# A bidirectional mLSTM and Fourier encoder block on one core: longer scans in the gate chain, an earlier load of half of w_out, and the residual of the last layer written during its passes

## Chip, core and metric

One core of a Trainium2 chip runs the whole block. The metric is the device time of one execution in microseconds (us), as the median of several runs. All arithmetic is float32; the matmuls work on float32 values that were split into a rounded part and a remainder (below).

## What is computed

Sequence 1024, model width 1024, one layer. Of the reference, cut to what matters here:

```python
sh1, sc1, g1, sh2, sc2, g2 = split(silu(c) @ w_ada + b_ada, 6)
h = ln_plain(x) * (1 + sc1) + sh1
q, k, v, o, fz, gates = split(h @ w_in)
# mLSTM, 4 heads, forward and backward in time, chunks of 128 positions:
#   b = cumsum(log_f) in the chunk; running maximum of (log_i - b) in the chunk;
#   then a recurrence over the 8 chunks with state C, n, m
y = concat(mlstm(q, k, v, gates) * sigmoid(o), real(fft2(fz)))
x = ln_affine(ALPHA * x + (1 + g1) * (y @ w_out), ln1_g, ln1_b)
h2 = ln_plain(x) * (1 + sc2) + sh2
ff = square(relu(h2 @ w_ff1 + b_ff1)) @ w_ff2 + b_ff2      # width 4096 inside
return ln_affine(ALPHA * x + (1 + g2) * ff, ln2_g, ln2_b)
```

## The kernel before

**Matmuls.** Each product is three matmuls into one PSUM bank (`mm3`, lines L133, L134, L135): rounded times rounded, rounded times remainder, remainder times rounded. An operand is loaded raw, cast by ACT into its rounded part, and DVE (or POOL) subtracts to get the remainder. FF1 and FF2 multiply blocks by a scheme with fewer products: sums and differences of blocks are formed, and FF2 runs as seven passes, numbered 1, 2, 5, 6, 3, 7, 4, of 8 units each. A unit is a left and a right operand (`split_op`, L1204 cast, L1205 subtraction) and 24 matmuls. Left operands are read back from a DRAM buffer `hid_d` (`left`, L1221, on ACT's queue), right ones come from w_ff2 (`w2_raw`, L1212, on SP's queue).

**What sets the order.** The text is recorded first, and each engine's instructions are then put into an order by a scheduler; an engine and a queue work strictly in that order. `issue_after` ties an instruction to another. Tiles of one tag share a few places (`bufs`), so a load waits until the last reader of the tile that was there is done. The raw loads of all stages share the tag "raw" with three places in pool `xp`.

**The gate chain (L449 to L526).** Gates of 4 heads and 2 directions stand as rows of 64 x 1024 tiles: `I` (input gate), `Fz` (forget gate). DVE forms log-sigmoid, 16 scans for the cumulated sum in each chunk and direction (L468, L470), a subtraction (L472), 16 scans for the running maximum (L476, L478), small steps over the 8 chunk ends (L489 to L499), then L507 and L506. PE transposes the result of L506 (L522). Meanwhile PE multiplies V and other projections.

**The output projection (L864 to L895).** `wo_load` brings a 128 x 512 row block of w_out's second column half, one load, cast (L822) and subtraction (L823) each, eight in all. `acc_load` reads the residual x, `gate_rows(0, g1)` reads the row of the gate g1 (from `gr_d`) and the bias row b_ada and combines them (L680). `wo_pass` multiplies, then DVE scales the bank by g1 (L891) and adds it to `acc` (L892), which frees the bank. PE's order has the second column half of row blocks 1 and 3 (`woh`, `wol`) ahead of row block 4.

**The last layer.** After FF2's pass 1, `gate_rows(1, g2)` and `gb` (b_ff2 times g2, L1344) are formed, and eight instructions (L1347) set `acc[st] = ALPHA * x + gb`.

Of the kernel before, what the change touches and what calls it, by code (L numbers as in the profile page):

```python
# [22 lines left out]
NC = 8  # L23
# [9 lines left out]
ALPHA = 2.0 ** 0.25  # L33
# [57 lines left out]
def body(ctx, tc, x, c, w_ada, b_ada, w_in, b_gate, norm_w, w_out, ln1_g, ln1_b,  # L91
         w_ff1, b_ff1, w_ff2, b_ff2, ln2_g, ln2_b, cst, dft, out):
    nc = tc.nc
# [4 lines left out]
    wout = w_out.rearrange("o (kt p) n -> p (o kt) n", p=P)  # L98
# [18 lines left out]
    xes, xp = pool("xp", "left")  # L117
# [87 lines left out]
    pt = bank("c")  # L205
# [245 lines left out]
    for k_, dst in ((1, Fz), (0, I)):  # L451
        for hf in range(2):
            pt = bank("c")
            for i in range(4):
                nc.tensor.transpose(out=pt[0:64, i * P:(i + 1) * P], in_=zg[:, hf * 4 + i, k_, :], identity=ident)
            nc.vector.tensor_copy(out=dst[0:64, hf * 512:hf * 512 + 512], in_=pt[0:64, :])
    on = ones.broadcast_to([P, P])
    e_ = rowt("e_", 3)[0:64]
    Fr = Fz[0:64]
# [3 lines left out]
    nc.scalar.activation(out=e_, in_=e_, func=AF.Ln, bias=1.0)  # L463
    nc.vector.scalar_tensor_tensor(out=Fr, in0=Fr, scalar=0.0, in1=e_, op0=ALU.min, op1=ALU.subtract)
    br = e_
    for n in range(NC):
        f, r_ = slice(n * P, n * P + P), slice(n * P + P - 1, n * P - 1 if n else None, -1)
        nc.vector.tensor_tensor_scan(out=br[0:32, f], data0=on[0:32], data1=Fr[0:32, f], initial=0.0,  # L468
                                     op0=ALU.mult, op1=ALU.add)
        nc.vector.tensor_tensor_scan(out=br[32:64, r_], data0=on[32:64], data1=Fr[32:64, r_], initial=0.0,  # L470
                                     op0=ALU.mult, op1=ALU.add)
    nc.vector.tensor_sub(out=a_, in0=a_, in1=br)  # L472
    cm = Fr
    for n in range(NC):
        f, r_ = slice(n * P, n * P + P), slice(n * P + P - 1, n * P - 1 if n else None, -1)
        nc.vector.tensor_tensor_scan(out=cm[0:32, f], data0=a_[0:32, f], data1=a_[0:32, f], initial=-3e38,  # L476
                                     op0=ALU.max, op1=ALU.max)
        nc.vector.tensor_tensor_scan(out=cm[32:64, r_], data0=a_[32:64, r_], data1=a_[32:64, r_], initial=-3e38,  # L478
                                     op0=ALU.max, op1=ALU.max)
    G = a2.tile([64, NC], F32, name="G")  # L480
    bL = a2.tile([64, NC], F32, name="bL")
    ms = p0.tile([64, NC + 1], F32, name="ms")
# [19 lines left out]
    def bcn(t_):  # L502
        return t_.unsqueeze(2).broadcast_to([64, NC, P])

    a_v = a_.rearrange("p (n t) -> p n t", t=P)
    nc.vector.tensor_tensor(out=I[64:128].rearrange("p (n t) -> p n t", t=P), in0=a_v, in1=bcn(mx), op=ALU.subtract)  # L506
    nc.vector.tensor_tensor(out=cmv, in0=cmv, in1=bcn(m0), op=ALU.max)  # L507
    M = cm
    wi = rowt("wi", 0)[0:64]
    wiv = wi.rearrange("p (n t) -> p n t", t=P)  # L510
# [362 lines left out]
    def acc_load(st):  # L873
        nc.sync.dma_start(out=acc[st], in_=xv[:, st, :])

    for i in range(3):
        acc_load(i)
    gate_rows(0, g1)
    for kt in range(KT):
        wo_load(b1.tile([P, 512], F32R, name=f"woh{kt}"), b1.tile([P, 512], F32R, name=f"wol{kt}"), kt, 1, nc.vector)  # L880
    for i in range(3, NST):
        acc_load(i)

# [331 lines left out]
    nraw = [0]  # L1215

    def left(p, u):
        nraw[0] += 1
        pl, t_, n_ = ((r2, "hraw", 2), (opp, "op4", 2))[nraw[0] // 2 % 2] if nraw[0] > 2 else (xp, "raw", 3)
        raw = pl.tile([P, 2, 512], F32, name="hraw", tag=t_, bufs=n_)  # L1220
        nc.scalar.dma_start(out=raw, in_=hid_d[p - 1, 2 * u:2 * u + 2].rearrange("n p d -> p n d"))  # L1221
        return raw

    NU = NPR // 2
# [88 lines left out]
    for n_, p in enumerate((1, 2, 5, 6, 3, 7, 4)):  # L1313
        pbs = [bank(t_) for t_ in ("aabc", "abbc")[n_ % 2]]
        late = NLAST if p == 4 else 0
        for u in range(NU - late):
            ab = split_op(left(p, u), nc.vector), split_op(right(p, u), nc.vector)
            for i in range(4):
                mm_unit(pbs[i], i, u, ab)
            if p == 3:  # L1320
                raw = w2_raw(u, 1, 0)
                nc.vector.tensor_sub(out=tt[u], in0=raw, in1=tt[u])
            if p == 7 and u % 2:
                for ch in range(2):
# [12 lines left out]
        if n_ == 0:
            lg2, lb2 = [r2.tile([P, D], F32, name=n) for n in ("lg2", "lb2")]
            nc.sync.dma_start(out=lg2, in_=bc1(ln2_g))
            nc.sync.dma_start(out=lb2, in_=bc1(ln2_b))  # L1340
            gate_rows(1, g2)
            gb = xp.tile([P, D], F32, name="gb", tag="raw", bufs=3)
            nc.sync.dma_start(out=gb, in_=bc1(b_ff2))
            nc.vector.tensor_mul(out=gb, in0=gb, in1=g2)  # L1344
            for st in range(NST):
                nc.sync.dma_start(out=acc[st], in_=x2_d[st * P:st * P + P, :])
                nc.vector.scalar_tensor_tensor(out=acc[st], in0=acc[st], scalar=ALPHA, in1=gb, op0=ALU.mult,  # L1347
                                               op1=ALU.add)
# [25 lines left out]
```

## Time and profile before

| | |
|---|---|
| three runs | 1107.94, 1109.8, 1109.94 us; median 1109.8 |
| profiled execution | 1109.07 us, of it 1107.3 us from the first to the last instruction (the span), 1.8 us around it |
| PE (matmuls) | 1042.8 us busy, 94% |
| DVE / ACT / POOL | 775.9 (70%) / 469.4 (42%) / 319.6 us (29%) |
[...]

The engines: PE multiplies, DVE, ACT and POOL work elementwise, SP and ACT issue DMAs. A row of the timeline gives start, duration, engine, line, operation, output and inputs with shapes, a count, and in brackets the idle time before it and what ended it. [...] A busy PE at 0.50 does half the work.

### The profile page before, as it was taken

How to read it: one execution, taken by the hardware profiler on the slowest of the kernel's cores; microseconds unless marked ns; L12 is line 12 of the kernel's file. 1: busy time of each engine (PE TensorE's matmuls, PEld its weight loads, DVE VectorE, ACT ScalarE, POOL GpSimd, SP SyncE). 2: the span in 40 equal slices, each digit the busy share in tenths (PEclk: the TensorE clock that was granted, in tenths of full speed). 3: DMA queues.
4: the chain of work that ended last, by engine and by line, in shares of the span. 5: the costliest groups of instructions: out<-in, count | busy, mean ns of one | idle time of the engine just before them, and what ended most of it. 6: DMA issues, size and time to landing. Idle time of an engine off the chain costs nothing.

```text
span 1107.3 us, 14282 instructions
## 1 busy us (share of the span) xinstructions
PE 1042.8 (94%) x5033; PEld 857.1 (77%) x5033; DVE 775.9 (70%) x1431; ACT 469.4 (42%) x812; POOL 319.6 (29%) x247
## 2 busy tenths in 40 slices
PE   5899989999899898879999999999989999999995
PEld 3788978898677687668888888888868888888884
DVE  7943785967779488878565445445476896668997
ACT  3353125654355115676455445354344333333420
POOL 3554205532124011002777766752200000000000
PEclk7999989989899899989999999999999999999998
DMA  9926604432224802854566564546978885688402
GB/s 307 290 60 216 195 28 122 132 115 89 82 65 137 284 39 102 251 180 125 162 212 206 180 206 150 178 152 204 340 282 288 266 308 190 218 271 282 163 30 93
DMA packets 146887, 199.31 MB, mean 180 GB/s; under 512 B 9392, under 2 KB 74876, under 8 KB 146816
## 3 DMA queue, kind: packets, MB, share of 16 engines
q1 hardware_dynamic: 126688, 162.22, 44.7%
q10 hardware_dynamic: 20128, 36.18, 9.7%
q8 instruction: 39, 0.64, 0.2%
q14 instruction: 32, 0.26, 0.1%
HBM read 153.01 MB, written 45.36 MB: 179 GB/s over the span
## 4 chain that ended last, share of the span: by engine, by line
PE 57%; DVE 2%; ACT 1%; DMA 0%; issue 0%; DVEq 0%; ACTq 0%
PE psb L134 7%; PE psb L135 7%; PE psb L133 7%; PE psa L133 7%; PE psa L134 7%; PE psa L135 7%; PE psc L134 5%; PE psc L135 5%; PE psc L133 5%; DVE acc L1347 0%; PE psc L933 0%; DMA rw<-in_w_ff_dram 0%; DVE acc L1304 0%; ACT b L937 0%; ACT w L955 0%
## 5 line engine op out<-in xcount | busy, mean ns | idle before, releaser
L1204 ACT CAST o<-hraw 128x1024 fp32r<-128x1024 f32 x56 | 58.6, 1050 | 137.1 <-PE psc L135 107.5
L1205 DVE TENSOR_TENSOR o<-hraw,o 128x1024 fp32r<-128x1024 f32 x56 | 70.5, 1265 | 42.2 <-ACT o L1204 42.2
L133 PE MATMUL psa<-wh,hR 128*128 128x256 f32 (+2 forms) x268 | 81.0, 303 | 0.6 <-DVE acc L892 0.6
L135 PE MATMUL psa<-wh,hR 128*128 128x256 f32 (+2 forms) x268 | 79.9, 298 | 0.0
L134 PE MATMUL psa<-wl,hR 128*128 128x256 f32 (+2 forms) x268 | 79.4, 297 | 0.0
L134 PE MATMUL psa<-o,o 128*128 128x512 f32 x176 | 69.3, 394 | 5.9 <-DVE o L1205 5.9
L135 PE MATMUL psa<-o,o 128*128 128x512 f32 x176 | 69.4, 394 | 0.0
L133 PE MATMUL psa<-o,o 128*128 128x512 f32 x176 | 68.9, 393 | 0.0
L978 ACT ACTIVATE hq<-hq 128x512 f32<-128x512 f32 x59 | 37.1, 629 | 62.2 <-DVE hq L974 61.4
L134 PE MATMUL psb<-o,o 128*128 128x512 f32 x160 | 62.9, 393 | 0.0
L135 PE MATMUL psb<-o,o 128*128 128x512 f32 x160 | 62.8, 393 | 0.0
L133 PE MATMUL psb<-o,o 128*128 128x512 f32 x160 | 62.4, 392 | 0.0
L263 POOL TENSOR_TENSOR wl<-raw,wh 128x256 fp32r<-128x256 f32 (+2 forms) x27 | 38.0, 1430 | 73.8 <-ACT wh L262 73.8
L133 PEld LDWEIGHTS psa<-wh,hR 128*128 128x128 f32 x268 | 52.6, 196 | 2.7 <-DVE acc L892 1.3
L134 PEld LDWEIGHTS psa<-wl,hR 128*128 128x128 f32 x268 | 52.6, 196 | 2.0 <-issue 0.9
L135 PEld LDWEIGHTS psa<-wh,hR 128*128 128x128 f32 x268 | 52.4, 196 | 1.0
L1047 DVE TENSOR_TENSOR ws<-raw,ws 128x1024 fp32r<-128x1024 f32 x30 | 39.6, 1333 | 13.8 <-ACT ws L1046 13.8
L418 POOL TENSOR_TENSOR m<-m,mraw 128x512 f32<-128x512 f32 x28 | 39.5, 1412 | 29.6 <-ACT m L415 10.3
L1037 POOL TENSOR_TENSOR raw<-raw 128x512 f32<-128x512 f32 x15 | 21.3, 1418 | 90.4 <-DVE w L1112 86.2
L1204 ACT CAST o<-raw 128x1024 fp32r<-128x1024 f32 x32 | 33.3, 1048 | 31.4 <-DVE raw L1247 18.2
L1171 POOL TENSOR_TENSOR hq<-hq 128x512 f32<-128x512 f32 x16 | 22.7, 1418 | 78.1 <-ACT hq L979 62.1
L134 PEld LDWEIGHTS psa<-o,o 128*128 128x128 f32 x176 | 33.3, 189 | 13.7 <-DVE o L1205 6.3
(437 smaller groups left out, 3150.6 us busy)
## 6 DMA issues: line engine op xcount, KB each, us to landing
raw<-in_w_ff_dram SPq DMA_DIRECT2D x104, 512.0 KB, 4.8
hraw<-hid_d ACTq DMA_DIRECT2D x56, 512.0 KB, 4.8
hid_d<-hq SPq DMA_DIRECT2D x107, 256.0 KB, 3.2
mraw<-in_w_ada_dram SPq DMA_DIRECT2D x32, 512.0 KB, 4.2
raw<-in_w_in_dram SPq DMA_DIRECT2D x10, 512.0 KB, 3.9
xt<-in_x_dram SPq DMA_DIRECT2D x8, 512.0 KB, 5.3
wa<-in_w_ada_dram SPq DMA_DIRECT2D x16, 256.0 KB, 5.2
wa<-in_w_ada_dram SPq DMA_DIRECT2D x8, 512.0 KB, 8.1
```

Source lines behind the costliest of these rows:

```text
L133: nc.tensor.matmul(out=out_ap, lhsT=lh, rhs=rh, start=first, stop=False)
L134: nc.tensor.matmul(out=out_ap, lhsT=lh, rhs=rl, start=False, stop=False)
L135: return nc.tensor.matmul(out=out_ap, lhsT=ll, rhs=rh, start=False, stop=last)
L263: nc.gpsimd.tensor_sub(out=wl, in0=raw, in1=wh)
L418: nc.gpsimd.tensor_add(out=mc, in0=mc, in1=rv[:, i])
L978: nc.scalar.activation(out=h_, in_=h_, func=AF.Relu)
L1037: eng.tensor_add(out=r1[:, hi], in0=r1[:, lo], in1=r1[:, hi])
L1047: nc.vector.tensor_sub(out=w_[:, 1], in0=s_, in1=w_[:, 0])
L1171: nc.gpsimd.tensor_add(out=sa, in0=h12, in1=h22)
L1204: nc.scalar.copy(out=o_[:, 0], in_=raw)
L1205: eng.tensor_sub(out=o_[:, 1], in0=raw, in1=o_[:, 0])
```

## The change

Three places are edited. In the gate chain the 32 scans of 32 x 128 become 4 of 32 x 1024: a tile `keep` (two planes of 64 x 1024, set by POOL) holds, as the multiplier or addend of each position, 1 and 0 (sum) or 0 and -3e38 (maximum), so that the scan starts anew at each chunk. Two of the four copies at L456 go from DVE to ACT, and the maximum with m0 is tied behind the subtraction of mx. In the output projection four loads of two row blocks each replace eight of one; three of them stand ahead of the residual and the gate row. In FF2 the residual is written inside passes 2 and 5, `gb` has a tile of its own, `lb2` takes its place before pass 6, and `left` issues on SP's queue from its fourth call on, with other places.

```diff
@@ gate chain
-            nc.vector.tensor_copy(out=dst[0:64, ...], in_=pt[0:64, :])
+            (nc.vector.tensor_copy if k_ else nc.scalar.copy)(out=dst[0:64, ...], in_=pt[0:64, :])
...
-    for n in range(NC):
-        f, r_ = slice(n * P, n * P + P), slice(n * P + P - 1, n * P - 1 if n else None, -1)
-        nc.vector.tensor_tensor_scan(out=br[0:32, f], data0=on[0:32], data1=Fr[0:32, f], initial=0.0,
-                                     op0=ALU.mult, op1=ALU.add)
-        nc.vector.tensor_tensor_scan(out=br[32:64, r_], ...)
+    keep = md.tile([64, 2, S], F32, name="keep")
+    for w_, (rest, start) in enumerate(((1.0, 0.0), (0.0, -3e38))):
+        nc.gpsimd.memset(keep[:, w_], rest)
+        nc.gpsimd.memset(keep[:, w_].rearrange("p (n t) -> p n t", t=P)[:, :, 0:1], start)
+
+    def scans(out, src, which, initial, op0, op1):
+        for rs, r_ in ((slice(0, 32), slice(None)), (slice(32, 64), slice(None, None, -1))):
+            nc.vector.tensor_tensor_scan(out=out[rs, r_], data0=keep[rs, which], data1=src[rs, r_], initial=initial,
+                                         op0=op0, op1=op1)
+
+    scans(br, Fr, 0, 0.0, ALU.mult, ALU.add)
     nc.vector.tensor_sub(out=a_, in0=a_, in1=br)
     cm = Fr
-    for n in range(NC):
...
+    scans(cm, a_, 1, -3e38, ALU.add, ALU.max)
...
-    nc.vector.tensor_tensor(out=I[64:128]..., in0=a_v, in1=bcn(mx), op=ALU.subtract)
-    nc.vector.tensor_tensor(out=cmv, in0=cmv, in1=bcn(m0), op=ALU.max)
+    i_op = nc.vector.tensor_tensor(out=I[64:128]..., in0=a_v, in1=bcn(mx), op=ALU.subtract)
+    with tc.issue_after(i_op.ins):
+        nc.vector.tensor_tensor(out=cmv, in0=cmv, in1=bcn(m0), op=ALU.max)
@@ output projection
+    wor = {}
+    def wo_raw(j):
+        wor[j] = xp.tile([P, 2, 512], F32, name="wraw", tag="raw", bufs=3)
+        nc.sync.dma_start(out=wor[j], in_=wout[:, 2 * j:2 * j + 2, 512:1024])
+    for j in range(3):
+        wo_raw(j)
...
     for i in range(3):
         acc_load(i)
+    for kt in range(KT):
+        if kt == 6:
+            wo_raw(3)
+        a_, b_ = [b1.tile([P, 512], F32R, name=f"wo{n_}{kt}") for n_ in "hl"]
+        nc.scalar.copy(out=a_, in_=wor[kt // 2][:, kt % 2])
+        nc.vector.tensor_sub(out=b_, in0=wor[kt // 2][:, kt % 2], in1=a_)
+        wo[1][kt] = a_, b_
     gate_rows(0, g1)
-    for kt in range(KT):
-        wo_load(b1.tile(... f"woh{kt}"), b1.tile(... f"wol{kt}"), kt, 1, nc.vector)
@@ FF2
-        pl, t_, n_ = ((r2, "hraw", 2), (opp, "op4", 2))[nraw[0] // 2 % 2] if nraw[0] > 2 else (xp, "raw", 3)
+        pl, t_, n_ = ((opp, "op4", 2), (r2, "hraw", 2))[nraw[0] // 2 % 2 == 0] if nraw[0] > 1 else (xp, "raw", 3)
...
-        nc.scalar.dma_start(out=raw, in_=hid_d[...])
+        (nc.scalar if nraw[0] <= 3 else nc.sync).dma_start(out=raw, in_=hid_d[...])
...
+            if p in (2, 5) and u % 2:
+                st = u // 2 + (4 if p == 5 else 0)
+                nc.sync.dma_start(out=acc[st], in_=x2_d[st * P:st * P + P, :])
+                nc.vector.scalar_tensor_tensor(out=acc[st], in0=acc[st], scalar=ALPHA, in1=gb, op0=ALU.mult,
+                                               op1=ALU.add)
...
-        if n_ == 0:
-            lg2, lb2 = [r2.tile([P, D], F32, name=n) for n in ("lg2", "lb2")]
-            ...
-            gb = xp.tile([P, D], F32, name="gb", tag="raw", bufs=3)
-            ...
-            for st in range(NST):
-                (load of acc[st], scalar_tensor_tensor as above)
+        if p == 1:
+            gate_rows(1, g2)
+            gb = r2.tile([P, D], F32, name="gb", tag="gb", bufs=1)
+            (load of b_ff2, multiplication by g2, as before)
+        if p == 6:
+            lg2 = r2.tile([P, D], F32, name="lg2")
+            lb2 = r2.tile([P, D], F32, name="lb2", tag="gb", bufs=1)
+            (loads of both)
```

**Order on PE at the transposes of I.** `wh_...`, `wl_...` are the weights of a projection; the transposes read `I`. Before:

```order
L133 MATMUL psa<-wh_1393,hR 128x256
L134 MATMUL psa<-wl_1394,hR 128x256
L135 MATMUL psa<-wh_1393,hR 128x256
L522 MATMUL psc<-cs,I 128x128 x8
L133 MATMUL psa<-wh_2638,hR 128x256
```

Now:

```order
L135 MATMUL psa<-wh_1370,hR 128x256
L133 MATMUL psa<-wh_1370,hR 128x256
L525 MATMUL psc<-cs,I 128x128 x8
L134 MATMUL psa<-wl_1371,hR 128x256
L135 MATMUL psa<-wh_1370,hR 128x256
L133 MATMUL psa<-wh_1370,hR 128x256
```

Before, the transposes follow the last of the V projection's matmuls (`wh_1393`); now 29 matmuls of the same projection (`wh_1370` there) stand behind them.

**Order on SP's queue in the output projection.** `wraw` is w_out, `raw` the bias row, `lg` the norm's weight, `acc` the residual, `g` the gate row. Before:

```order
L821 DMA wraw<-in_w_out_dram 128x512 x2
L874 DMA acc_3719<-in_x_dram 128x1024
L874 DMA acc_3720<-in_x_dram 128x1024
L874 DMA acc_3721<-in_x_dram 128x1024
L677 DMA g_3730<-gr_d 128x1024
L874 DMA acc_3722<-in_x_dram 128x1024
L821 DMA wraw<-in_w_out_dram 128x512 x2
```

Now:

```order
L872 DMA wraw<-in_w_out_dram 128x2x512
L682 DMA raw<-in_b_ada_dram 128x1024
L918 DMA lg<-in_ln_g_dram 128x1024
L885 DMA acc_3702<-in_x_dram 128x1024
L885 DMA acc_3703<-in_x_dram 128x1024
L885 DMA acc_3704<-in_x_dram 128x1024
L680 DMA g_3713<-gr_d 128x1024
L885 DMA acc_3705<-in_x_dram 128x1024
```

The bias row stood seven loads of w_out and sg earlier and `lg` behind all of it; now both stand between the last load of w_out and the residual, ahead of the gate row.

**Order on DVE at the end of FF2's pass 1.** `o<-hraw` is the subtraction for a left operand, `o<-raw` for a right one. Before:

```order
L1205 TENSOR_TENSOR o_7529<-hraw,o_7529 128x1024
L1205 TENSOR_TENSOR o_7495<-hraw,o_7495 128x1024
L1205 TENSOR_TENSOR o_7563<-hraw,o_7563 128x1024
L680 SCALAR_TENSOR_TENSOR g_7173<-g_7173,raw 128x1024
L1344 TENSOR_TENSOR gb<-gb,g_7173 128x1024
L1347 SCALAR_TENSOR_TENSOR acc_7149<-acc_7149,gb 128x1024
...
L1347 SCALAR_TENSOR_TENSOR acc_7156<-acc_7156,gb 128x1024
L1205 TENSOR_TENSOR o_7500<-raw,o_7500 128x1024
```

Now:

```order
L1221 TENSOR_TENSOR o_7444<-hraw,o_7444 128x1024
L1221 TENSOR_TENSOR o_7478<-hraw,o_7478 128x1024
L683 SCALAR_TENSOR_TENSOR g_7142<-g_7142,raw 128x1024
L1362 TENSOR_TENSOR gb<-gb,g_7142 128x1024
L1221 TENSOR_TENSOR o_7514<-hraw,o_7514 128x1024
L1342 SCALAR_TENSOR_TENSOR acc_7118<-acc_7118,gb 128x1024
...
L1342 SCALAR_TENSOR_TENSOR acc_7125<-acc_7125,gb 128x1024
L1221 TENSOR_TENSOR o_7449<-raw,o_7449 128x1024
```

The gate row and `gb` moved ahead of the third left operand of pass 2; all eight residual instructions still stand in one row, behind that operand and ahead of pass 2's first right operand (`o_7500` before, `o_7449` now).

## Rows read from the trace of the kernel before

**Rows 1.** The page's first part: busy time, share of the span and instructions per engine.

```profile
PE 1042.8 (94%) x5033; PEld 857.1 (77%) x5033; DVE 775.9 (70%) x1431; ACT 469.4 (42%) x812; POOL 319.6 (29%) x247
```

**Rows 2.** Waits of PE: line, releaser, us in total, times, longest.

```profile
PE psa L134 <- DVE o L1205: 5.9, 1, 5.9
...
PE psc L522 <- DVE I L506: 5.4, 1, 5.4
```

**Rows 3.** Window of the gate chain: length, busy per engine, PEclk, DMA share, GB/s.

```profile
164.00:166.00 2.00, 2.00 (x11) 2.00 (x11) 0.54 (x3) 2.00 (x4) 0.37 (x1) 0.50 0.00 0
```

**Rows 4.** Timeline of DVE, gate chain.

```profile
151.31 0.41 DVE L476 TENSOR_TENSOR_SCAN Fz<-I 32x128 f32<-32x128 f32 x1
...
158.17 0.35 DVE L489 COPY G<-Fz 32x8 f32<-32x8 f32 x2
158.56 0.16 DVE L492 TENSOR_TENSOR_SCAN ms<-G,bL 32x8 f32<-32x8 f32 x1
...
159.42 1.21 DVE L507 TENSOR_TENSOR Fz<-Fz,m 64x1024 f32<-64x1024 f32 x1
...
160.74 1.22 DVE L506 TENSOR_TENSOR I<-I,mx 64x1024 f32<-64x1024 f32 x1
```

**Rows 5.** Timeline of PE, end of the V projection and transposes of I.

```profile
156.24 0.28 PE L134 MATMUL psa<-wl,hR 128*128 128x256 f32 x1
156.36 0.28 PE L135 MATMUL psa<-wh,hR 128*128 128x256 f32 x1
162.01 1.97 PE L522 MATMUL psc<-cs,I 128*128 128x128 f32 x8 [5.37 <-DVE I L506]
```

**Rows 6.** Timeline of POOL, behind its memset of zg (91.32 to 92.29).

```profile
95.80 0.29 POOL L371 CAST selq<-cs 128x128 fp32r<-128x128 f32 x1 [3.52 <-DMA so_d<-so]
```

**Rows 7.** Timeline of PE, output projection (first row: its second column half begins).

```profile
366.66 0.39 PE L133 MATMUL psa<-woh,hR 128*128 128x512 f32 x1
366.89 0.40 PE L134 MATMUL psa<-wol,hR 128*128 128x512 f32 x1
...
375.05 1.22 PE L133 MATMUL psa<-woh,hR 128*128 128x512 f32 x2 [2.77 <-ACT woh L822]
376.83 0.79 PE L133 MATMUL psa<-wh,hR 128*128 128x512 f32 x1 [0.56 <-DVE acc L892]
```

**Rows 8.** Windows, output projection and the first norm behind it.

```profile
366.00:370.00 4.00, 4.00 (x19) 3.31 (x18) 0.21 (x1) 0.00 (x0) 0.00 (x0) 1.00 0.99 372
...
378.00:380.00 2.00, 2.00 (x7) 1.51 (x6) 2.00 (x4) 0.00 (x0) 0.00 (x0) 0.50 0.69 249
...
405.00:420.00 15.00, 15.00 (x67) 12.30 (x66) 15.00 (x37) 2.24 (x7) 3.70 (x2) 1.00 0.26 105
...
428.00:432.00 4.00, 1.27 (x6) 0.40 (x4) 3.10 (x13) 3.94 (x6) 0.15 (x1) 1.00 0.00 0
```

**Rows 9.** Timelines of SP's queue (first row) and DVE, output projection.

```profile
363.49 0.51 SPq L677 DMA_DIRECT2D g<-gr_d  x1
...
372.37 1.23 DVE L680 SCALAR_TENSOR_TENSOR g<-g,raw 128x1024 f32<-128x1024 f32 x1 [6.17 <-DMA g<-gr_d]
...
391.21 0.70 DVE L891 TENSOR_TENSOR psb<-psb,g 128x512 f32<-128x512 f32 x1 [8.40 <-PE psb L135]
```

**Rows 10.** Timeline of DVE, end of FF2's pass 1.

```profile
818.02 1.22 DVE L680 SCALAR_TENSOR_TENSOR g<-g,raw 128x1024 f32<-128x1024 f32 x1
...
820.54 9.17 DVE L1347 SCALAR_TENSOR_TENSOR acc<-acc,gb 128x1024 f32<-128x1024 f32 x8
829.62 1.22 DVE L1205 TENSOR_TENSOR o<-raw,o 128x1024 fp32r<-128x1024 f32 x1
```

**Rows 11.** SP's queue there, landing of its DMA (785 to 830), its waits from 830.

```profile
807.71 0.33 SPq L679 DMA_DIRECT2D raw<-in_b_ada_dram  x1
...
gb<-in_b_ff_dram SPq DMA_DIRECT2D x1, 512.0 KB, 6.7
...
SPq L1212 <- DVE o L1205: 67.0, 22, 19.9
```

More of the change, by code (lines that the diff above doesn't have):

```diff
@@ L455, in body @@
                 nc.tensor.transpose(out=pt[0:64, i * P:(i + 1) * P], in_=zg[:, hf * 4 + i, k_, :], identity=ident)
-            nc.vector.tensor_copy(out=dst[0:64, hf * 512:hf * 512 + 512], in_=pt[0:64, :])
+            (nc.vector.tensor_copy if k_ else nc.scalar.copy)(out=dst[0:64, hf * 512:hf * 512 + 512], in_=pt[0:64, :])
     on = ones.broadcast_to([P, P])
@@ L465, in body @@
     br = e_
-    for n in range(NC):
-        f, r_ = slice(n * P, n * P + P), slice(n * P + P - 1, n * P - 1 if n else None, -1)
-        nc.vector.tensor_tensor_scan(out=br[0:32, f], data0=on[0:32], data1=Fr[0:32, f], initial=0.0,
-                                     op0=ALU.mult, op1=ALU.add)
-        nc.vector.tensor_tensor_scan(out=br[32:64, r_], data0=on[32:64], data1=Fr[32:64, r_], initial=0.0,
-                                     op0=ALU.mult, op1=ALU.add)
+    keep = md.tile([64, 2, S], F32, name="keep")
[7 more added lines that the diff above has]
+    scans(br, Fr, 0, 0.0, ALU.mult, ALU.add)
     nc.vector.tensor_sub(out=a_, in0=a_, in1=br)
     cm = Fr
-    for n in range(NC):
[L475 to L479, printed above, removed]
+    scans(cm, a_, 1, -3e38, ALU.add, ALU.max)
     G = a2.tile([64, NC], F32, name="G")
@@ L505, in body @@
     a_v = a_.rearrange("p (n t) -> p n t", t=P)
-    nc.vector.tensor_tensor(out=I[64:128].rearrange("p (n t) -> p n t", t=P), in0=a_v, in1=bcn(mx), op=ALU.subtract)
-    nc.vector.tensor_tensor(out=cmv, in0=cmv, in1=bcn(m0), op=ALU.max)
+    i_op = nc.vector.tensor_tensor(out=I[64:128].rearrange("p (n t) -> p n t", t=P), in0=a_v, in1=bcn(mx),
+                                   op=ALU.subtract)
+    with tc.issue_after(i_op.ins):
+        nc.vector.tensor_tensor(out=cmv, in0=cmv, in1=bcn(m0), op=ALU.max)
     M = cm
@@ L877, in body @@
         acc_load(i)
+    for kt in range(KT):
[5 more added lines that the diff above has]
+        wo[1][kt] = a_, b_
     gate_rows(0, g1)
-    for kt in range(KT):
-        wo_load(b1.tile([P, 512], F32R, name=f"woh{kt}"), b1.tile([P, 512], F32R, name=f"wol{kt}"), kt, 1, nc.vector)
     for i in range(3, NST):
@@ L1218, in left @@
         nraw[0] += 1
-        pl, t_, n_ = ((r2, "hraw", 2), (opp, "op4", 2))[nraw[0] // 2 % 2] if nraw[0] > 2 else (xp, "raw", 3)
+        pl, t_, n_ = ((opp, "op4", 2), (r2, "hraw", 2))[nraw[0] // 2 % 2 == 0] if nraw[0] > 1 else (xp, "raw", 3)
         raw = pl.tile([P, 2, 512], F32, name="hraw", tag=t_, bufs=n_)
-        nc.scalar.dma_start(out=raw, in_=hid_d[p - 1, 2 * u:2 * u + 2].rearrange("n p d -> p n d"))
+        (nc.scalar if nraw[0] <= 3 else nc.sync).dma_start(out=raw, in_=hid_d[p - 1, 2 * u:2 * u + 2].rearrange("n p d -> p n d"))
         return raw
@@ L1336, in body @@
                 ln2(4 + i)
-        if n_ == 0:
-            lg2, lb2 = [r2.tile([P, D], F32, name=n) for n in ("lg2", "lb2")]
+        if p == 1:
+            gate_rows(1, g2)
+            gb = r2.tile([P, D], F32, name="gb", tag="gb", bufs=1)
+            nc.sync.dma_start(out=gb, in_=bc1(b_ff2))
+            nc.vector.tensor_mul(out=gb, in0=gb, in1=g2)
+        if p == 6:
+            lg2 = r2.tile([P, D], F32, name="lg2")
+            lb2 = r2.tile([P, D], F32, name="lb2", tag="gb", bufs=1)
             nc.sync.dma_start(out=lg2, in_=bc1(ln2_g))
             nc.sync.dma_start(out=lb2, in_=bc1(ln2_b))
-            gate_rows(1, g2)
-            gb = xp.tile([P, D], F32, name="gb", tag="raw", bufs=3)
-            nc.sync.dma_start(out=gb, in_=bc1(b_ff2))
-            nc.vector.tensor_mul(out=gb, in0=gb, in1=g2)
-            for st in range(NST):
-                nc.sync.dma_start(out=acc[st], in_=x2_d[st * P:st * P + P, :])
-                nc.vector.scalar_tensor_tensor(out=acc[st], in0=acc[st], scalar=ALPHA, in1=gb, op0=ALU.mult,
-                                               op1=ALU.add)
 _INS = ["x", "c", "w_ada", "b_ada", "w_in", "b_gate", "mlstm_norm_w", "w_out", "ln1_g", "ln1_b",
```

## Prediction

> **What bounds the kernel.** I read the busy times first: PE works 1042.8 of 1107.3 us [rows 1], so 64.5 us of the span are PE's idle time, and what can be won is that and the half clock behind it. Then the waits of PE, to see which of the three edited places still holds one, then for each the timeline of the engine that PE waits for. All three hold one, and DVE ends each: 5.4 us for I, 5.9 us for an operand of FF2's pass 2 [rows 2], 2.77 + 0.56 us in the output projection, for a cast and for a bank [rows 7]. Behind the first, PE works at 0.50 until about 166 [rows 3], so of the 4 us from 162.01 it loses half, 2.0. In the third its two matmuls at 375.05 take 0.61 each in place of 0.39 [rows 7] and the clock is still 0.50 until 380 [rows 8], a loss of about 2.5. Behind the second I assume 2.0 like the first (an estimate). Together 14.6 us of idle time and 6.5 us of clock: about 21 us is the ceiling at the three places.
>
> **A, the gate chain.** The second set of 16 scans takes 158.17 − 151.31 = 6.86 us [rows 4]; the first has the same forms and I count the same. Four scans of 32 x 1024 replace them, a width that the trace does not show for a scan. From 8 to 128 columns a scan grows from 0.16 to 0.41 [rows 4], 2.08 ns a column, so one of 1024 costs 0.41 + 896 x 2.08 ns = 2.27 us, two 4.55. The nearest row of that width, L507, says 1.21, two 2.42; eight old ones in a row say 3.28, two 6.56. I take 2.27, as it comes from scans. This saves 2 x (6.86 − 4.55) = 4.6 us; L507 behind L506 saves 1.2 more. I is ready 5.8 us earlier, at 161.96 − 5.8 = 156.2.
>
> [...]
>
> But PE comes earlier too: 29 matmuls stood ahead of the transposes and now stand behind. At 0.12 us each [rows 5] that is 3.5, so PE stands there at 156.64 − 3.5 = 153.1 and waits 3.1 us instead of 5.37. The gain is 2.3. A wait of 2.77 was enough for the half clock elsewhere [rows 7, 8], so I keep those 2.0. Ends: with scans of 1.21, I comes at about 152, no wait and no half clock, 7.4; with 3.28, I at 158.2, a wait of 5.1, 0.3. The memsets of `keep` lie in POOL's gap of 3.52 us [rows 6]; without that gap they would push POOL's casts by some 2 us, which PE need not see. The two copies moved to ACT lie beside DVE's work on Fz; at nothing.
>
> **B, the output projection.** Before, PE works 24 matmuls of row blocks 1 and 3 and waits for the fifth block of w_out [rows 7]. Now the whole of both is loaded ahead, 48 matmuls at 0.23 (366.66 to 366.89 [rows 7]) from 366.66, so PE reaches row block 4 at 377.7 without that wait. It then needs the bank of row block 0, which needs the gate row. That row was issued at 363.49 and used at 372.37 [rows 9]; the bank was free 4.46 later (376.83 [rows 7]). Now the bias row and `lg`, 512 KB each, stand ahead of it. At 372 GB/s with the DMA share at 0.99 [rows 8] they cost 2.8 us, so the row is there at 375.2, and with one more L891 (0.6) the bank is free at 380.3. PE waits 2.6 us in place of 3.33, and keeps the half clock: a gain of 0.7. Ends: if the loads start so early that the row comes at 372.4, no wait is left and 5.8 is won; if SP holds the row 2 us more for a place of the raw tag, the wait is 4.6 and 1.3 is lost.
>
> Something else follows. DVE is idle for 8.4 us until 391.21 [rows 9], then full at 15.00 of 15.00 [rows 8], and PE stands 2.7 of 4 us at 428 to 432 [rows 8] for the norm's results. With row blocks 1 and 3 done by 378, DVE can start their second halves and statistics inside that gap. If all of it arrives, 2.7 us go and the half clock behind it, some 1.5 (an estimate from the other places), 4.2; if the last tile's own chain sets the end, nothing. I take half, 2.1. B: 2.8, from −1.3 to 10.
>
> **C, the residual.** DVE's row is: third left operand, gate row at 818.02, `gb`, eight times 1.15 us (9.17), then the right operand that PE waits for, at 829.62 [rows 10]; PE resumes at 830.90. The change names passes 2 and 5, but in the new order all eight still stand in one row ahead of that operand. Only the gate row and `gb` now stand ahead of the third left operand. The bias row bounds the gate row: issued at 807.71, and a load beside it took 6.7 [rows 11], so about 814.4. Then gate 815.6, `gb` 816.8, third operand 818.1, eight residuals 827.3, right operand 828.5: 2.4 earlier than 830.84. PE's wait shrinks from 5.9 to 3.5, the half clock stays. Ends: bias row so early that the third operand alone (PE frees its place two units of 24 x 0.23 = 5.5 us ahead of the wait's start at 825, at 814; cast and subtraction to 816.5) sets the start, a wait of 1.8, and no half clock: 6; bias row behind left loads that now stand on SP's queue ahead of it, 2.4 later: 0. The residuals' work itself is not less, and no later pass waits.
>
> **Sum.** 2.3 + 2.8 + 2.4 = 7.5 us from the profiled run's 1109.07 gives 1101.6. The median is 0.7 above that run, so 1102.3; I forecast 1102, at the place where most of the stalls shrink and none goes.
>
> **Rivals.**
>
> *The stalls go.* Each term at its good end: 7.4 + 10 + 6 = 23, some 1086; with two of three, about 1092. For it: every stall is only about 3 us after the change, and one that falls a little further takes the half clock along, so gains come in steps of 4 to 5. Against: three estimates would have to be off in one direction. 0.25, at 1086 to 1097.
>
> *The stalls move.* The transposes stand earlier, the gate row later, the eight residuals stay together: 0.3 − 1.3 + 0 = −1.0 at the bad ends; with one term as forecast, a gain of 1 to 3, 1106 to 1109. What speaks for it is that the order on the engines shows each of the three. 0.22.
>
> *Slower, by SP's queue.* From the fourth left operand on, SP's queue carries lefts, rights, stores and `lb2` in one order. It already waits 67.0 us in 22 times for DVE's subtraction, up to 19.9 [rows 11]. A left load behind such a wait needs some 6.7 us to land [rows 11] and 2.4 for its split (1.22 for the subtraction [rows 10], as much for the cast), 9.1 in all. A unit takes PE 5.5 us, and if two units are ready ahead, 11 us are covered. So a wait of more than 1.9 us ahead of a left load begins to stall PE; one of 19.9 would cost 18 us and 2 of clock, 20 − 7.5 = 12.5 slower, 1122. From 1.9 + 7.5 + 2.2 − 2 = 9.6 us on such a wait decides. Against: DVE's longest waits lie where the raw tiles are ahead of need, and before, ACT's queue held the lefts in order too. 0.13, at 1112 to 1122.
>
> [...]
>
> *It doesn't do what it says.* For the residual that is already in the order (above) and in the sum.
>
> **Numbers.** Forecast, 1097 to 1106: 0.40. Stalls go: 0.25. Stalls move: 0.22, of it a third inside 0.2% (2.2 us, about what a measurement of this kernel can tell from no change). Slower: 0.13. Faster by over 0.2%: 0.40 + 0.25 + 0.14 = 0.79; same 0.08; slower 0.13. The range must leave out 0.2 at most: from 1091 (a third of the case above is left out) to 1109 (the slower case and a little of the same are left out).
>
> **What would show it.** After: PE's wait for I 3 us and ahead of the projection's last 29 matmuls; scans of 2.2 to 2.4 us. A scan near 1.2 or a wait at zero raises A to 7. PE's wait for `woh` gone, one of 2 to 4 us for a bank at row block 4, the gate row landing at about 375 on this clock. DVE busy at 382 to 391, PE's gaps at 428 smaller. Eight residuals in a row and a wait of 3 to 4 us for the right operand of pass 2. ACT without the waiting issues of lefts, and SP's waits without an idle PE in passes 5 to 4; a PE wait there for a left operand makes the third rival true. Wrong would make it, above all, a changed order in the recurrence behind the gate chain or in FF1, whose stalls I hold constant.

## The result, and the profile after

The changed kernel takes 1098.87 us (median of four runs, 1094.95 to 1099.49) against 1109.5 us for the kernel before: a ratio of 0.9899, 95% interval 0.9874 to 0.9924. That is 10.6 us faster by the medians and 11.2 by the ratio (8.4 to 14.0 by its interval). The forecast was 1102, with a range of 1091 to 1109.

The first part of the page of the changed kernel answers [rows 1]: PE is busy for 1039.9 of 1097.7 us, so 57.8 us are idle, 6.7 less than before. The other 2.9 us of the 9.6 by which the span shrank are shorter matmuls, since the mean granted clock rose from 0.965 to 0.972 of full speed. DVE has 9.0 us less work.

PEclk, the granted clock of PE as a share of full speed, is 1.00 or 0.50 in the windows of both traces, and between them where a window lies across a switch. In the kernel before, the 128 x 512 matmuls behind the waits of [rows 7] begin 0.43 us apart at 0.50 (377.43 to 380.41) and 0.23 apart at 1.00 (381.46 to 382.83): at the half clock PE does 0.53 of the work.

```profile
PE 1039.9 (95%) x5033; PEld 853.2 (78%) x5033; DVE 766.9 (70%) x1401; ACT 469.6 (43%) x814; POOL 321.1 (29%) x251
```

The waits of PE in the changed kernel (line, releaser, us in total, times, longest) answer [rows 2]:

```profile
PE psc L525 <- DVE I L507: 3.4, 1, 3.4
...
PE psa L133 <- DVE acc L908: 2.7, 1, 2.7
...
PE psa L134 <- DVE o L1221: 1.9, 1, 1.9
PE psa L133 <- ACT w L1127: 1.6, 1, 1.6
...
PE psa L135 <- DVE w L1128: 0.8, 1, 0.8
```

The wait for I fell from 5.4 to 3.4, that for the operand of pass 2 from 5.9 to 1.9, and a wait of 2.7 for the bank took the place of 2.77 + 0.56 in [rows 7]. The last two rows, in FF1, are new.

The three places on the timelines of the changed kernel: DVE in the gate chain (compare [rows 4]), SP, DVE and PE in the output projection (compare [rows 7, 9]), DVE and PE at the end of FF2's pass 1 (compare [rows 10]).

```profile
143.01 4.59 DVE L474 TENSOR_TENSOR_SCAN e__1287<-keep,Fz 32x1024 f32<-32x1024 f32 x2
...
155.30 1.22 DVE L507 TENSOR_TENSOR I<-I,mx 64x1024 f32<-64x1024 f32 x1
...
156.57 0.69 PE L525 MATMUL psc<-cs,I 128*128 128x128 f32 x2 [3.37 <-DVE I L507]
```

```profile
360.46 1.08 SPq L680 DMA_DIRECT2D g<-gr_d  x1
...
369.68 1.23 DVE L683 SCALAR_TENSOR_TENSOR g<-g,raw 128x1024 f32<-128x1024 f32 x1 [8.07 <-DMA g<-gr_d]
...
374.74 0.79 PE L133 MATMUL psa<-wh,hR 128*128 128x512 f32 x1 [2.69 <-DVE acc L908]
...
386.87 0.70 DVE L907 TENSOR_TENSOR psb<-psb,g 128x512 f32<-128x512 f32 x1 [6.82 <-PE psb L135]
```

```profile
807.31 1.23 DVE L683 SCALAR_TENSOR_TENSOR g<-g,raw 128x1024 f32<-128x1024 f32 x1 [2.69 <-DMA raw<-in_b_ada_dram]
...
810.99 9.17 DVE L1342 SCALAR_TENSOR_TENSOR acc<-acc,gb 128x1024 f32<-128x1024 f32 x8
820.07 2.35 DVE L1221 TENSOR_TENSOR o<-raw,o 128x1024 fp32r<-128x1024 f32 x2
...
821.34 0.50 PE L134 MATMUL psa<-o,o 128*128 128x512 f32 x1 [1.95 <-DVE o L1221]
```

Two scans of 32 x 1024 take 4.59 us, 2.3 each; the gate row is used 9.22 us after its issue; the eight residuals still stand in one row.

Where PE stands at the start of five stages, by its own timeline in each trace, in us:

| first matmul of | before | changed | ahead by |
|---|---|---|---|
| the Fourier products with U (L768, L771) | 286.88 | 279.06 | 7.8 |
| second half of w_out | 366.66 | 361.00 | 5.7 |
| FF1's first transposes | 422.30 | 415.92 | 6.4 |
| FF2's pass 1 | 780.12 | 774.52 | 5.6 |
| PE's last matmul starts | 1095.37 | 1085.45 | 9.9 |

The gate chain and the recurrence behind it give more than the whole of what is left at the end of FF1; the output projection adds under 1 us, which FF1 takes back; FF2 adds 4.3. Single traces scatter. In the three kernels with the gate chain of before and its order on PE, the products with U begin at 285.25, 285.48 and 286.88. In the eight kernels with the changed chain and its order on PE, they begin between 277.76 and 281.45. So the table gives places, good to some 2 us, and the times of several runs give the sizes; the gain of the chain at U is clear of this scatter.

### The profile page after: what moved, and what is told of

Its sections match the earlier page's. It is cut to its first block, busy times and chain, and to the rows that moved or that the text cites. A ratio compares the mean times of both kernels' runs of the same rounds, so it can differ in the third digit from the quotient of the medians.

```text
span 1097.7 us, 14279 instructions
## 1 busy us (share of the span) xinstructions
PE 1039.9 (95%) x5033; PEld 853.2 (78%) x5033; DVE 766.9 (70%) x1401; ACT 469.6 (43%) x814; POOL 321.1 (29%) x251
## 4 chain that ended last, share of the span: by engine, by line
PE 71%; DVE 13%; DMA 7%; issue 3%; ACT 2%; POOL 1%; SPq 1%; DVEq 0%; ACTq 0%; POOLq 0%
PE psa L134 10%; PE psa L133 9%; PE psa L135 9%; PE psb L134 7%; PE psb L135 7%; PE psb L133 7%; PE psc L134 5%; PE psc L135 5%; PE psc L133 5%; DVE macc L308 2%; DMA wa<-in_w_ada_dram 2%; DMA hid_d<-eh 1%; PE psb L646 1%; PE psb L637 1%; DMA g<-gr_d 1%
## 5 line engine op out<-in xcount | busy, mean ns | idle before, releaser
L133 PE MATMUL psa<-wh,hR 128*128 128x256 f32 (+2 forms) x268 | 80.0, 299 | 2.7 <-DVE acc L908 2.7
L135 PE MATMUL psa<-wh,hR 128*128 128x256 f32 (+2 forms) x268 | 78.5, 293 | 0.0
L418 POOL TENSOR_TENSOR m<-m,mraw 128x512 f32<-128x512 f32 x28 | 37.1, 1328 | 34.3 <-ACT m L415 19.4
L1221 DVE TENSOR_TENSOR o<-raw,o 128x1024 fp32r<-128x1024 f32 x32 | 39.8, 1251 | 8.3 <-ACT o L1220 8.0
```

Of the source, the lines that this page charges most:

```text
L133: nc.tensor.matmul(out=out_ap, lhsT=lh, rhs=rh, start=first, stop=False)
L135: return nc.tensor.matmul(out=out_ap, lhsT=ll, rhs=rh, start=False, stop=last)
L418: nc.gpsimd.tensor_add(out=mc, in0=mc, in1=rv[:, i])
L1221: eng.tensor_sub(out=o_[:, 1], in0=raw, in1=o_[:, 0])
```

## The experiments

In all of them the ratio is to the kernel before on the same chip, whose median was 1109.1, 1109.4 and 1109.1 us in the three groups. A gain over the kernel before is worked out from this ratio. A gain over the changed kernel is a difference of medians from different chips, and below some 4 us it lies inside the two intervals: there the trace has to bear it out.

### Each part by itself

The kernel before with one of the three edits of the diff each: the gate chain, the output projection, FF2.

> Of the change only the gate chain (four long scans, the copies on ACT, the subtraction of mx first). Theory: PE's wait for I falls from 5.37 to about 3.4 us as in the changed kernel, with the half clock kept, and the waits for kw behind it (1.58 and 0.51) go, as I and its columns come 5.5 us earlier: 4 to 6 us faster than before, 1103.5 to 1105.5. Rival: the gain behind the gate chain came from the other order in the recurrence that the scheduler chose because of the other two parts; then this kernel gains only 2 to 2.5 us, 1107.

Measured: 1101.62 us, ratio 0.9931 (0.9914 to 0.9948), 7.6 us faster. More than either theory. PE reaches the products with U already at 278.82, and its waits between 150 and 290 us are, in this kernel

```profile
PE psc L525 <- DVE I L507: 3.4, 1, 3.4
PE psc L609 <- DVE qw L601: 2.5, 1, 2.5
PE psb L637 <- ACT tb L664: 2.3, 1, 2.3
...
PE psb L569 <- DVE kw L562: 0.3, 1, 0.3
```

and in the kernel before

```profile
PE psc L522 <- DVE I L506: 5.4, 1, 5.4
PE psb L634 <- ACT tb L661: 3.0, 1, 3.0
PE psc L606 <- DVE qw L598: 2.1, 1, 2.1
PE psc L555 <- DVE kw L559: 1.6, 1, 1.6
PE psb L566 <- DVE kw L559: 0.5, 1, 0.5
...
```

The two waits for kw are one of 0.3 us now. The half clock behind the wait for qw is shorter too. The windows (length, busy per engine, then PEclk) of this kernel, and below of the kernel before:

```profile
214.00:216.00 2.00, 2.00 (x10) 1.91 (x11) 1.94 (x4) 0.37 (x1) 1.92 (x2) 0.69 0.61 226
216.00:218.00 2.00, 2.00 (x12) 2.00 (x10) 1.60 (x7) 0.30 (x2) 0.60 (x1) 0.50 0.63 205
218.00:220.00 2.00, 2.00 (x14) 1.56 (x13) 1.76 (x7) 2.00 (x5) 0.00 (x0) 0.96 0.37 127
```

```profile
218.00:220.00 2.00, 1.99 (x10) 1.77 (x11) 2.00 (x2) 0.20 (x1) 1.92 (x2) 0.50 0.83 214
...
226.00:228.00 2.00, 2.00 (x11) 1.86 (x11) 0.00 (x0) 1.33 (x2) 0.80 (x1) 0.61 0.76 168
```

Some 4 us at 0.50 instead of 10, so 3 us less lost. About half of that is scatter: in the kernel with the output projection alone, whose chain is that of before, the clock is at 0.50 for some 7 us (218 to 224 and a part of the windows beside). The columns of I feed kw, the state and qw on DVE, and all of that comes earlier.

> Of the change only the output projection (four loads of 512 KB ahead of residual and gate row). Theory: PE's 2.77 us for the cast of w_out go, a wait of 2.5 to 3 us for the bank at row block 4 takes the place of 0.56, and the waits at the end of the first norm shrink: 1.5 to 4 us faster, 1105.5 to 1108. If this part is also what causes the waits of FF1 that the changed kernel has at 523 to 525 (1.63 and 0.81 us and some 1.5 us of half clock), it is 0 to 1 us faster. Rival: the bank's wait costs as much as the cast's and nothing is won, 1109 to 1110.

Measured: 1109.36 us, ratio 1.0001 (0.9986 to 1.0016). Nothing is won. The rival has the number but not the cause: the wait for the bank is 2.4 us, near the expected, in place of 3.33, and PE reaches FF1's transposes 0.8 us sooner after the start of the second half than before. Then FF1 takes most of it back (358.4 us from its first transposes to pass 1, against 357.8), as the second case of the expectation had it. Its waits between 350 and 540 us show the two operands of FF1 (`w`, from ACT's and DVE's splits at L1124 and L1125) that the kernel before does not wait for:

```profile
PE psa L135 <- DVE w L1125: 1.9, 2, 1.0
...
PE psa L133 <- ACT w L1124: 1.5, 1, 1.5
```

> Of the change only FF2 (left operands on SP's queue, gate row and its product ahead of the third left operand, a tile of its own for the product). Theory: PE's wait for the first right operand of pass 2 falls from 5.90 to about 2 us, the half clock behind it stays, nothing else moves: 3.5 to 4.5 us faster, 1105 to 1106. Rival: the wait is as long as before when nothing ahead of it has moved, because the bias row lands as late as before: 0 to 2 us faster.

Measured: 1104.16 us, ratio 0.9952 (0.9937 to 0.9967), 5.3 us faster. PE's wait for the operand is 2.01 us, 3.9 less, and the clock behind it stays up. These are the windows of this kernel behind its wait (at 826.90), and below those of the fully changed kernel behind its 1.95 us:

```profile
826.00:828.00 2.00, 1.10 (x5) 0.93 (x6) 2.00 (x3) 0.47 (x1) 0.00 (x0) 1.00 0.60 190
828.00:830.00 2.00, 2.00 (x10) 1.63 (x9) 2.00 (x2) 0.00 (x0) 0.00 (x0) 1.00 0.86 285
```

```profile
820.00:822.00 2.00, 0.66 (x3) 0.51 (x4) 2.00 (x3) 0.97 (x2) 0.00 (x0) 0.95 0.29 106
822.00:824.00 2.00, 2.00 (x6) 1.61 (x5) 2.00 (x3) 0.00 (x0) 0.00 (x0) 0.50 0.84 193
```

In the kernel before, the clock is at 0.50 from the end of the wait (830.90) to about 835, so some 2 of the 5.3 us are the half clock that is gone. The three gains add to 7.6 − 0.1 + 5.3 = 12.8 us; together they measured 11.2 by the same ratio. The difference of 1.6 lies inside the intervals. The traces show two pieces that would make it, the half clock just shown and FF1's waits: the kernel with the gate chain alone starts pass 1 at 772.63, the fully changed one at 774.52.

### What in the gate chain won

The kernel before with the two small edits of the chain, the short scans kept (order only):

```diff
-            nc.vector.tensor_copy(out=dst[0:64, ...], in_=pt[0:64, :])
+            (nc.vector.tensor_copy if k_ else nc.scalar.copy)(out=dst[0:64, ...], in_=pt[0:64, :])
...
+    with tc.issue_after(i_op.ins):
+        nc.vector.tensor_tensor(out=cmv, in0=cmv, in1=bcn(m0), op=ALU.max)
```

> The kernel before, with only the two small edits of the gate chain: the copies of I on ACT and the subtraction of mx ahead of the maximum, the 32 short scans kept. The whole gate chain alone won 7.5 us, where the prediction had 2.3. Theory: the gain comes from the 4.6 us that the long scans take off DVE's chain, and what is left here is 1.2 us at most: 1108 to 1109. Rival: the earlier transposes and the order behind them are what won, then this kernel wins 3 us or more.

Measured: 1112.23 us, ratio 1.0031 (1.0011 to 1.005), 3.4 us slower. The small edits by themselves win nothing; the gain needs the long scans. Without them nine matmuls stand behind the transposes of I, PE does these 0.6 us earlier (161.37 against 162.01) after a wait as long as before, and it waits longer for qw:

```profile
PE psc L524 <- DVE I L506: 5.4, 1, 5.4
PE psc L608 <- DVE qw L600: 4.0, 1, 4.0
...
```

PE reaches the products with U at 287.00, level with the kernel before. Where the 3.4 us are lost is not shown.

Then the changed kernel with the transposes of I behind all of the V projection:

```diff
+    (the V projection, with v0_mm = its last matmul, moved here from behind the transposes)
     for hf in range(2):
...
+            with tc.issue_after(v0_mm.ins):
                 nc.tensor.transpose(out=pt[:, i * P:(i + 1) * P], in_=I[:, n * P:(n + 1) * P], identity=ident)
```

> The changed kernel, with the V projection written ahead of the transposes of I and the transposes tied behind its last matmul, so that the 29 matmuls that stood behind them cover the wait. Theory: the wait of 3.37 us for I falls to 0 to 0.3 us and the half clock behind it (some 1.5 us) goes; the columns of I come no later than before, so nothing new waits: 3.5 to 5 us faster than the changed kernel, 1094 to 1095.5. Rival: the matmuls that were behind the transposes covered the next steps (the transposes of e, kw), and the wait moves there: within 1 us of 1098.9.

Measured: 1098.99 us, ratio 0.9909 (0.9891 to 0.9928): nothing against 1098.87. PE does not wait for I at all in this kernel, but for the next steps, between 150 and 290 us:

```profile
PE psb L642 <- ACT tb L669: 2.3, 1, 2.3
PE psc L563 <- DVE kw L567: 2.1, 1, 2.1
PE psc L614 <- DVE qw L606: 2.1, 1, 2.1
PE psb L642 <- DVE C L586: 1.5, 1, 1.5
PE psc L541 <- ACT wk L538: 0.8, 1, 0.8
...
```

All waits of that stretch add up to 9.8 us, against 9.2 in the changed kernel. PE reaches the products with U at 279.17, as before this edit (279.06). The theory fell and the rival holds: the wait moves along the chain. In this kernel all of the V projection stands ahead of the transposes, as in the kernel before, and the gain is there all the same. So the long scans make it, and not the place of the transposes.

### The gate row and the place of row block 4

The changed kernel with the gate row loaded ahead of the residual:

```diff
+    gate_rows(0, g1)
     for i in range(3):
         acc_load(i)
...
-    gate_rows(0, g1)
```

> The changed kernel, with the gate row and its bias row loaded ahead of the residual instead of behind its first three loads. Theory: the bank of row block 0 waits for the gate row, which came 9.2 us after its issue behind 1.5 MB of residual and 0.5 MB of lg; now it lands 4 to 5 us earlier and the wait of 2.69 us at row block 4 goes, with its half clock of some 1.2 us: 2.5 to 4 us faster than the changed kernel, 1095 to 1096.5. Rival: the residual is then late by as much, since the bank is freed only after it has been added to the residual: no gain, within 1 us of 1098.9.

Measured: 1089.85 us, ratio 0.9828 (0.9806 to 0.985), 9.0 us faster than the changed kernel and more than twice what was expected. SP issues the row and DVE uses it at

```profile
356.21 0.42 SPq L680 DMA_DIRECT2D g<-gr_d  x1
...
363.58 1.23 DVE L683 SCALAR_TENSOR_TENSOR g<-g,raw 128x1024 f32<-128x1024 f32 x1 [2.41 <-DMA g<-gr_d]
```

PE does not wait at all until FF1. The scheduler also moved row block 4 behind the second halves of all four row blocks, 48 matmuls later, and FF1's waits changed. From 350 to 530 us:

```profile
PE psc L949 <- ACT xn2q L161: 5.1, 1, 5.1
PE psa L135 <- DVE w L972: 3.3, 2, 2.2
PE psc L949 <- ACT b L953: 3.0, 3, 1.1
...
```

To separate the two, the changed kernel with that order on PE and the gate row late:

```diff
+                wo_12 = (last matmul of the second half of row block 2)
...
             for st in sts:
-                wo_pass(0, st)
+                with tc.issue_after(wo_12.ins):
+                    wo_pass(0, st)
```

> The changed kernel, with row block 4 of the output projection tied behind the second column half of all four row blocks on PE; the loads keep the changed kernel's order, the gate row behind lg and three residual loads. With the gate row loaded first the scheduler had made just this order on PE, and that kernel is 9 us faster than the changed one. If the place of row block 4 on PE is the cause, because 48 more matmuls (10.9 us) then cover the gate row, this kernel is as fast, 1089 to 1091. If the early gate row is the cause, as DVE can work on the freed banks 5 us earlier, this one gains only the wait of 2.69 us and its half clock, 3 to 4.5 us: 1094 to 1096.

Measured: 1092.25 us, ratio 0.9846 (0.983 to 0.9862), 6.6 us faster than the changed kernel, between the two expectations. The expectation was wrong in one point: the second half of row block 0, which now comes first, needs a freed bank as well, so the wait is still there (3.44 us at 376.07). The gain is in FF1, which needs 354.2 us from its first transposes to pass 1 (415.85 to 770.09) instead of 358.6; PE's waits there add up to 10.8 us instead of 15.1. From 350 to 530 us:

```profile
PE psc L953 <- ACT xn2q L161: 5.1, 1, 5.1
PE psb L133 <- DVE acc L910: 3.4, 1, 3.4
...
```

The stretch from the start of the second half of w_out to pass 1 separates the two. It takes 413.5 us in the changed kernel, 408.5 in this one (361.58 to 770.09) and 406.2 with the gate row first (358.36 to 764.51). So the place of row block 4 won 5.0 us, and the early gate row another 2.4, about the wait for the bank (the two kernels' intervals overlap). With this order DVE's gap ahead of the second halves of row blocks 0 and 2 shrinks from 6.82 to 2.56 us, so the norm of row blocks 0 to 3 starts sooner; that FF1 waits less for this reason fits, but no run shows it by itself. The rest of both gains, 1.6 and 1.3 us, lies in FF2, which neither edit touches: PE waits for the first right operand of pass 2 about as long as in the changed kernel (1.9 and 2.2 us), but without the half clock behind it. With row block 4 late, the matmuls there begin 0.23 us apart (817.18 to 822.31), against 0.43 in the changed kernel (822.00 to 824.56). With the gate row first, the three groups of FF2's matmuls into `psa` take a mean of 391, 392 and 392 ns, as with FF2 alone; in the changed kernel they take 392, 394 and 393.

And the early gate row without the larger loads of w_out:

```diff
 (gate chain and FF2 as changed; output projection as before)
+    gate_rows(0, g1)
     for i in range(3):
         acc_load(i)
-    gate_rows(0, g1)
```

> The gate chain and FF2 as changed, the output projection with the eight single loads of before, but the gate row and bias row loaded ahead of the residual. Theory: the early loads of w_out are needed too, since PE otherwise waits for the casts of its fifth block as before (2.8 us and half clock) and takes row block 4 early: within 2 us of the kernel with gate chain and FF2 alone (some 1097 by their single gains, 1109.1 - 7.5 - 5.0). Rival: the early gate row alone makes the gain and the larger loads nothing: 1088 to 1091.

Measured: 1092.6 us, ratio 0.985 (0.9826 to 0.9873): 2.7 us behind the kernel with the larger loads, and about 4 ahead of what gate chain and FF2 give alone by their sum. Neither expectation held whole. In this kernel PE no longer waits for the cast of w_out's fifth block, only 0.85 us for a bank at 366.26, since the gate row frees banks early and other work comes first. From the start of the second half to pass 1 it needs 409.1 us, 2.9 more than with the larger loads, so these are worth some 2.7 us with the gate row early (by the trace; the intervals overlap), and nothing by themselves with it late.

### FF2: the queue and the row of eight

The changed kernel with `left` on ACT's queue for all calls:

```diff
-        (nc.scalar if nraw[0] <= 3 else nc.sync).dma_start(out=raw, in_=hid_d[...])
+        nc.scalar.dma_start(out=raw, in_=hid_d[...])
```

> The changed kernel with all left operands of FF2 issued on ACT's queue again, all else as changed. Theory: the left operands came earlier at the end of pass 1 because SP's queue issues them without ACT's waits; on ACT's queue the third left operand and the gate row come as late as before, PE waits 3.5 to 4 us instead of 1.95: 1.5 to 2.5 us slower than the changed kernel, 1100.5 to 1101.5. Rival: the queue does not matter, only the order on DVE does: within 0.7 us of the changed kernel's 1098.9. Second rival, the slower case of the prediction: SP's queue costs time in later passes, then this kernel is faster than the changed one.

Measured: 1096.18 us, ratio 0.9879 (0.9865 to 0.9894), 2.7 us faster than the changed kernel; its passes of FF2, from the first matmul of pass 1 to the last of pass 4, take 308.6 us against 310.9. My theory fell. The gate row did come later, as it said (812.07), but the wait is 1.09 us and the clock stays at 1.00 from 816 to 834. The timeline of DVE shows why: the scheduler put one right operand, the first of pass 2, ahead of the eight, and only the second behind them, so PE has one more unit of work before it waits.

```profile
814.47 1.22 DVE L1221 TENSOR_TENSOR o<-raw,o 128x1024 fp32r<-128x1024 f32 x1
815.60 9.17 DVE L1342 SCALAR_TENSOR_TENSOR acc<-acc,gb 128x1024 f32<-128x1024 f32 x8
824.69 1.21 DVE L1221 TENSOR_TENSOR o<-raw,o 128x1024 fp32r<-128x1024 f32 x1
```

It does not show that SP's queue costs time in later passes: PE waits nowhere else in FF2 in either kernel, though from 830 on SP waits 75.8 us in 37 times, up to 5.8, for a left operand's place in the changed one.

The changed kernel with the residuals really spread, each tied behind the subtraction of its unit's right operand:

```diff
+        o_sub[0] = eng.tensor_sub(out=o_[:, 1], in0=raw, in1=o_[:, 0])
...
+                with tc.issue_after(o_sub[0].ins):
                     nc.vector.scalar_tensor_tensor(out=acc[st], in0=acc[st], scalar=ALPHA, in1=gb, op0=ALU.mult,
```

> The changed kernel, with each residual instruction of FF2 tied behind the subtraction of its unit's right operand, so that four stand in pass 2 and four in pass 5 instead of eight in one row. Theory: the first right operand of pass 2 is ready about 9 us earlier and PE's wait of 1.95 us goes with its half clock of some 1.7 us: 2.5 to 4 us faster than the changed kernel, 1095 to 1096.5. Rival: DVE is near full later in these passes (38 of 40 us at 880 to 920), the spread work makes an operand late there: within 1 us, or slower.

Measured: 1094.12 us, ratio 0.9869 (0.9848 to 0.9891), 4.7 us faster than the changed kernel. PE waits nowhere in FF2 before the tail, and its passes take 307.2 us against 310.9. The rival, an operand late in the full stretch, did not come. DVE has one residual between operands:

```profile
817.49 1.23 DVE L1222 TENSOR_TENSOR o<-raw,o 128x1024 fp32r<-128x1024 f32 x1 [3.52 <-ACT o L1221]
818.63 1.22 DVE L1344 SCALAR_TENSOR_TENSOR acc<-acc,gb 128x1024 f32<-128x1024 f32 x1
819.77 1.22 DVE L1222 TENSOR_TENSOR o<-hraw,o 128x1024 fp32r<-128x1024 f32 x1
```

### Together

> The changed kernel with gate row first and residual spread, without the tied transposes of I. If the tied transposes are worth nothing, as alone, this is as fast as all three together: 1084.5 to 1086.5. If they are worth something once the other waits are gone, it is 1 to 3 us slower than that, 1086 to 1088.

Measured: 1087.58 us, ratio 0.9801 (0.9786 to 0.9817), 11.3 us faster than the changed kernel.

> The three edits together (transposes of I behind the projection, gate row first, residual spread). If the three waits are independent the gains add: 9 to 12 us faster than the changed kernel, 1087 to 1090. If they are not, because the time won is lost again in FF1's first blocks, whose waits (ACT's and DVE's operands, 12.7 us idle at 416 to 495) follow from DVE being full, the sum falls short: 1091 to 1094.

Measured: 1085.21 us, ratio 0.9786 (0.9769 to 0.9804): 13.7 us faster than the changed kernel, the best version here and better than either case expected. The expected limit in FF1 did not hold. The gate row and the residual together win 11.3 us of the 9.0 and 4.7 that they win alone; the half clock behind pass 2's wait, which is in both single gains, can go only once. Against the version without the tied transposes this one is 2.4 us faster, though alone they were worth nothing. That the transposes do it is not shown: the two intervals overlap, and the trace of all three is ahead by 3.0 us already at U (278.49 against 281.45), where 281.45 is the latest of the eight starts named above. Whether they count stays open.

## Why the prediction was right, and where it was not

**The gate chain** was forecast at 2.3 us and measured 7.6 by itself. Its own steps held: a long scan was put at 2.27 us and took 2.28, about twice the 1.21 of L507, the row of that width in [rows 4]; I was ready at 156.5 against 156.2, PE waited 3.37 against 3.1, and the half clock stayed, for some 3 us (PEclk 0.55 at 156 to 158, 0.60 at 158 to 160). One end of the range was miscounted: scans of 3.28 us would save 0.6 + 1.2 us and bring I at 160.2, not 158.2, so that end is a loss of 1.7 instead of a gain of 0.3. The mis-sized step was to hold what comes behind constant, which the prediction itself named as its greatest danger. It costed the wait for I alone; the chain feeds kw, the state and qw, and there the two waits for kw (2.1 us, of which 0.3 is left) and 1.5 to 3 us of half clock went as well. The order-only kernel and the one with the transposes tied show it from both sides: what counts is when DVE's chain is done, not where PE happens to stand in it.

**The output projection** was forecast at 2.8 and measured −0.1 by itself (interval −1.8 to 1.6 by the ratio's ends), nothing. The first term, 0.7 for the cast's wait against the bank's, held: a wait of 2.69 against 2.6. The half clock was kept but ended sooner than in [rows 8], as these windows of the changed kernel show:

```profile
376.00:378.00 2.00, 2.00 (x6) 1.51 (x6) 2.00 (x4) 0.00 (x0) 0.00 (x0) 0.50 0.94 269
378.00:380.00 2.00, 2.00 (x10) 1.65 (x9) 2.00 (x4) 0.00 (x0) 0.00 (x0) 0.98 0.05 12
```

The second term, 2.1 for half of the norm's gap at 428, was wrong. DVE's gap ahead of 391 [rows 9] stayed, 6.82 us in the changed kernel against 8.40, as the banks that DVE waits for there are those of row blocks 0 and 2, which PE does behind row block 4. The waits behind the norm were 3.7 us instead of 3.2 (1.66 + 0.69 + 1.36), and two of FF1's operands came late. Getting at that gap took another order on PE, which the kernel with row block 4 late shows:

```profile
383.35 0.70 DVE L909 TENSOR_TENSOR psb<-psb,g 128x512 f32<-128x512 f32 x1 [2.56 <-PE psb L135]
```

**FF2** was forecast at 2.4, measured 5.3 by itself. The order was read rightly: all eight in one row, ahead of the first right operand. Two sizes were off. The bias row landed in time to use the gate at 807.31, which with pass 1 starting 5.6 us earlier is 812.9 on the clock of before, 1.5 sooner than the 814.4 of the sum; the third left operand stood ready at once, so the eight began at 816.6 on that clock instead of 818.1. And the half clock, which the sum kept, stayed away in the kernel with FF2 alone, though not in the fully changed one; after waits of 2.01 and 1.95 us that is chance, as far as these rows show.

**The sum**, 7.5 against 10.6, is thus two terms too small and one too large. That it came so near is in part luck, since these errors offset each other. Of the rivals, SP's queue did not stall PE. Its waits for a left operand's place reach 5.8 us, over the 1.9 at which the prediction let PE begin to stall, and PE does not wait. With the left operands back on ACT's queue the difference came from the order on DVE. The left operands land a median 4.8 us after issue in the kernel before, on ACT's queue, and in the changed one, on SP's. That stalls move rather than go was true for the output projection alone, and for the tied transposes.

## What to carry to other kernels

A wait shortened at the head of a chain of dependent steps was worth here what the whole chain won (7.6 us, of which the wait for I itself made 2.0), and covering the same wait with other work of PE was worth nothing here: ask when the last link is done. A load issued early paid only when the row that frees the banks came early too (2.7 us against nothing); put the small row that frees resources first. The larger part of the gain there, 5.0 us, came from another order on PE, which the scheduler chose by itself. And that a text spreads work over passes does not mean that the scheduler does: read the order, and tie each piece to an instruction of the same engine.

## What the hardware showed

Waits of almost the same length had different ends. After 1.9, 2.01 and 2.2 us idle at the same place (row block 4 late, FF2 alone, gate row first) no half clock followed, by the clock of the windows with FF2 alone (1.00) and by the matmul times above in the other two; after 1.95 us (fully changed) the clock fell to 0.50 (822 to 824) and cost some 1.6 us. So at this place the length of the wait does not tell whether the half clock comes, and a forecast from it is off by some 1.6 us either way. A scan on 32 partitions took 0.16 us for 8 columns, 0.41 for 128 and 2.28 for 1024: 2.08 ns a column from the first to the second, 2.09 from there to the third.
